# Differential attention in a four-layer trunk: value evacuation in pairs, a second room for the cast of queries and keys, rotation from the scaled copy, exponentials tied behind aT

## The chip, the cores and the metric

One Trainium2 chip (trn2), one of its cores. The metric is the device time of one execution in microseconds (us); smaller is better. All inputs and outputs are fp32. Matrix products are formed in three passes: each factor is split into a high part (type fp32r) and the low rest, and high x high, high x low and low x high are added up in PSUM.

## What is computed

The program is a trunk of four layers over a sequence of 512 tokens and 1024 channels; each has a mixer and a gated feed-forward part. The mixers are S5, gated linear attention, differential attention, S5. The change touches the third only, whose reference is, cut to its core:

```python
def diff_attn_mixer(h, positions, w_qkv, lam_q1, lam_k1, lam_q2, lam_k2, subln_g, w_o, lambda_init):
    q, k, v = jnp.split(h @ w_qkv, 3, axis=-1)
    q = partial_rope(q.reshape(bsz, seq, 16, 64), positions) * 64 ** -0.5
    k = partial_rope(k.reshape(bsz, seq, 16, 64), positions)
    v = v.reshape(bsz, seq, 8, 128)
...
        s = jnp.einsum('bqhd,bkhd->bhqk', qb, k)
        p = jax.nn.softmax(jnp.where(mask, s, NEG_INF), axis=-1)
        p = p.reshape(bsz, 8, 2, 128, seq)
        a = p[:, :, 0] - lam * p[:, :, 1]
        return jnp.einsum('bhqk,bkhd->bqhd', a, v)
...
    o = o * lax.rsqrt(jnp.mean(o * o, axis=-1, keepdims=True) + 1e-5) * subln_g * (1.0 - lambda_init)
    return o.reshape(bsz, seq, 1024) @ w_o
```

There are 8 heads of two softmaxes each. partial_rope rotates the first 16 of every 64 channels by tables of cosines and sines of the position.

## The kernel before

Everything below lies in the method diff (L2171 to L2500) and the few helpers that it calls. The layer input hT stands transposed in SBUF as a high and a low half; r is the row factor of the norm that precedes the layer. A "unit" is three matmuls (high x high, high x low, low x high) into one PSUM bank.

**Projections.** project(hf, z) computes 512 columns of queries (z = 0) or keys (z = 1) for half hf of the heads, in four banks of 128 tokens each (acc, four banks in all). When a bank is complete, evac empties it twice: ACT writes the copy scaled by r (qtm, L2237), and DVE reads the bank again for the rotation (ro, L2242 with cosines, L2245 twice with sines, from tables cos2r and sin2r that carry r already, made at L2205), and puts the rotated 16 columns into qtm (L2248). Six units later TensorE transposes qtm (L2253), and ACT copies the result to qk (L2254). Values for the first four heads come from project(0, 2); those for the others from values_of (L2386), which puts two blocks of 128 tokens into one bank, 256 columns each, and has ACT empty each half as soon as it is complete (vall, L2391). At the last k the matmuls of the second half of the bank follow on those of the first.

**Preparing a head.** prepare(j) has ACT write the high half of queries and keys (hl, L2273, 128x1024), DVE the low half (L2274), and then POOL issue eight DMAs (qs, L2281, four of 128 KB; ks, L2282, four of 256 KB) that lay the two softmaxes' rows out for the score matmuls. hl has one room, but for head 1, which takes one from the pool of weight halves (whl, five rooms, which holds ks as well). The cast of the next head writes that room, so it waits for the eight DMAs that read it. Head 4 and those after it use the second half of the projections, which are made beside steps 0 to 9.

**The 32 steps.** Step i stands for head j = i // 4 and query block t = i % 4. In a step TensorE's order is: turned(i), four transposes of the probabilities a (aTp, L2321), copied by ACT (aT, L2323); values(i - 1), the product with the values (op, L2331), copied by ACT (o_s, L2334) and squared for the norm (junk, L2336); at t = 2, prepare(j + 2); then scores(i + 2), four matmuls (L2299), for each softmax a DVE pass that adds the mask and takes the minimum (L2303, with nm) and an exponential on ACT (pr, L2307), then DVE's small steps (L2309, L2310) and the combination of the two softmaxes (pr, L2314); last, beside[i] units of other products (projections, then values, then the output product wo, whose first columns are ready from the first heads on). When a head is complete, normalised(j) forms its norm on DVE (L2343, L2344), a power on POOL (L524), and scales o_s on DVE (L2347); two steps later done transposes it (oTp, L2354), which ACT and DVE split into oT (L529, L530). done stands in the middle of the units of its step; in step 30 it stands right behind the scores, ahead of the first pair of units for the output.

In PSUM, the banks are acc (four), s (two) and two slots for everything that is transposed, which aTp, op, oTp and qTp share.

**What sets the order.** TensorE runs this layer in the order written in the code (self.hand). ACT, DVE, POOL and SP run in an order that a scheduler sets at build time from its own costs, with due times for what has to go first; issue_after(x) tells it that an instruction stands behind x on its engine. The weight halves of the products (whl) are made by ACT (L405) and DVE (L413) out of the staged weights (wst).

**Behind the steps.** values(31), the norm of head 7, the pairs of output units for two token blocks, the last oT, the other two blocks, and then the feed-forward part of the layer.

Of the kernel before, what the change touches and what calls it, by code (L numbers as in the profile page):

```python
# [22 lines left out]
P = 128  # L23
# [302 lines left out]
class Trunk:  # L326
# [1844 lines left out]
    def diff(self, l, left, after):  # L2171
# [4 lines left out]
        with self.tc.tile_pool(name="diff", bufs=1) as p:  # L2176
# [18 lines left out]
                nc.sync.dma_start(sg[:], i["diff_subln"][0].partition_broadcast(P))  # L2195
                v.tensor_scalar_mul(sg[:], sg[:], 1.0 - LAMBDA_INIT)

            cos2 = p.tile([P, NT, 16], F32, name="cos2r")
            sin2 = p.tile([P, NT, 16], F32, name="sin2r")

            def factors():

                left.finish()
                for o, y in ((cos2, self.cos2), (sin2, self.sin2)):
                    v.tensor_tensor(o[:], y[:], r[:].unsqueeze(2).broadcast_to([P, NT, 16]), op=ALU.mult)  # L2205

            self.pend.append(factors)

            stat = lambda k, part, t: hT[part][:, k, t * P : (t + 1) * P]

# [21 lines left out]
            def project(hf, z):  # L2232
                qk = qks[hf]

                def evac(t, ps):
                    q = self.np_.tile([P, 512], F32, tag=("h", "hh")[t % 2], name="qtm", bufs=2)
                    nc.scalar.mul(q[:], ps[:], r[:, t : t + 1])  # L2237
                    s3 = ps[:].rearrange("p (h d) -> p h d", d=64)
                    q3 = q[:].rearrange("p (h d) -> p h d", d=64)
                    ro = p.tile([P, 2, 8, 16], F32, tag="ro", name="ro", bufs=2)  # L2240
                    c2 = cos2[:, t].unsqueeze(1).broadcast_to([P, 8, 16])
                    v.tensor_tensor(ro[:, 0], s3[:, :, 0:16], c2, op=ALU.mult)  # L2242
                    for y in range(2):
                        s1 = sin2[:, t, y * 8 : y * 8 + 8].unsqueeze(1).broadcast_to([P, 8, 8])
                        v.tensor_tensor(  # L2245
                            ro[:, 1, :, y * 8 : y * 8 + 8], s3[:, :, 8 - 8 * y : 16 - 8 * y], s1, op=ALU.mult
                        )
                    v.tensor_tensor(q3[:, :, 0:16], ro[:, 0], ro[:, 1], op=ALU.add)  # L2248

                    def turn():  # L2250
                        tp = self.tp("qTp")
                        for j in range(4):
                            nc.tensor.transpose(tp[:, j], q[:, j * P : (j + 1) * P], self.ident[:])  # L2253
                        nc.scalar.copy(qk[:, z, :, t * P : (t + 1) * P], tp[:])  # L2254

                    queue.append((clock[0] + 6, turn))

                def evac_v(t, ps):
                    nc.scalar.mul(vall[0][:, t, hf * 512 : (hf + 1) * 512], ps[:], r[:, t : t + 1])

                if z == 2 and not vall:
                    vall.append(self.xp.tile([P, NT, D], F32, tag="x", name="vall"))
                yield from self.gemm_units(stat, w, KT, z * D + hf * 512, evac_v if z == 2 else evac)
# [3 lines left out]
            def prepare(j):  # L2267


                room, bufs, tag = (self.wp, 5, "whl") if j == 1 else (p, 1, "hl")  # L2270
                hl = room.tile([P, 2, 2, SEQ], F32R, tag=tag, name="hl", bufs=bufs)
                src = qks[j // 4][:, :, j % 4]
                nc.scalar.copy(hl[:, 0], src)  # L2273
                v.tensor_tensor(hl[:, 1], src, hl[:, 0].bitcast(F32), op=ALU.subtract)  # L2274
# [15 lines left out]
            def scores(i):  # L2290
                j, t = divmod(i, NT)
                ts = slice(t * P, (t + 1) * P)
                qs, ks = ready[j]
                st = kept[j][0]
                pr, sums = [], self.sp.tile([P, 4], F32, tag="sums", name="sums", bufs=4)
                ss = [self.sbank("s"), self.sbank("s")]
                for m in range(2):
                    for z in range(2):
                        nc.tensor.matmul(ss[m][:], qs[:, m, ts], ks[:, m, z], start=z == 0, stop=z == 1)  # L2299
                for m in range(2):  # L2300
                    e = T("pr", 4)
                    nm = self.sp.tile([P, 1], F32, tag="nm", name="nm", bufs=4)
                    v.tensor_tensor_reduce(  # L2303
                        e[:], ss[m][:], mask[:, t], -0.125, 3e38, op0=ALU.add, op1=ALU.min, accum_out=nm[:]
                    )
                    sum_ = st[:, 0, t : t + 1] if m == 0 else sums[:, 1:2]
                    nc.scalar.activation(e[:], e[:], AF.Exp, scale=-1.0, bias=nm[:], accum_out=sum_)  # L2307
                    pr.append(e)
                v.reciprocal(sums[:, 2:3], sums[:, 1:2])  # L2309
                v.tensor_scalar(  # L2310
                    sums[:, 3:4], st[:, 0, t : t + 1], sums[:, 2:3], self.neglam[:], op0=ALU.mult, op1=ALU.mult
                )
                a = pr[0]
                v.scalar_tensor_tensor(a[:], pr[1][:], sums[:, 3:4], pr[0][:], op0=ALU.mult, op1=ALU.add)  # L2314
                soft[i] = a

            def turned(i):
                a = soft.pop(i)
                tp = self.tp("aTp")
                for kt in range(4):  # L2320
                    nc.tensor.transpose(tp[:, kt], a[:, kt * P : (kt + 1) * P], self.ident[:])  # L2321
                aT = p.tile([P, 4, P], F32, tag="aT", name="aT", bufs=2)
                nc.scalar.copy(aT[:], tp[:])  # L2323
                return aT

            def values(i, aT):
# [48 lines left out]
            def values_of(c0):  # L2375

                banks = [self.acc(), self.acc()]
                for kb in range(0, KT, 4):
                    src = w[kb * P : (kb + 4) * P, 2 * D + c0 : 2 * D + c0 + 256]
                    hl = self.weights(src.rearrange("(a p) n -> p a n", p=P), 4, 256)  # L2380
                    for a in range(4):
                        k = kb + a
                        for t in range(NT):
                            o = banks[t // 2][:, (t % 2) * 256 : (t % 2 + 1) * 256]
                            for n, (x, y) in enumerate(((0, 0), (0, 1), (1, 0))):
                                nc.tensor.matmul(  # L2386
                                    o, stat(k, x, t), hl[:, y, a], start=not (k or t % 2 or n),
                                    stop=k == KT - 1 and n == 2, skip_group_check=True,
                                )
                            if k == KT - 1:  # L2390
                                nc.scalar.mul(vall[0][:, t, c0 : c0 + 256], o, r[:, t : t + 1])  # L2391
                            if t % 2:
                                yield

# [30 lines left out]
            def pair(k):  # L2425
                for t in range(2):
                    unit(t, k)
# [3 lines left out]
            for i in range(32):  # L2431
# [12 lines left out]
                if i < 30:  # L2444
                    scores(i + 2)
                if i == 30:
                    done.pop(i)()
                    banks = [self.sbank("acc1"), self.sbank("acc1")]
                    pair(0)
                run(units, beside[i] // 2)  # L2450
                if i in done:
                    done.pop(i)()
                run(units, beside[i] - beside[i] // 2)
                if i == 16:
                    back(0)
                if i == 20:
# [4 lines left out]
            values(31, aT)  # L2461
            last_head = normalised(7)
            back(1)
            for k in range(1, KT - 1):
                if k == KT - 2:
                    last_head()
                pair(k)
# [78 lines left out]
```

## Time and profile before

| | |
|---|---|
| three runs | 2276.57 us median (2271.59 to 2281.54) |
| profiled execution | 2276.01 us, of which the span is 2274.2 us |
| mean granted TensorE clock | 0.995 |
| attention layer | about 1150 to 1427 us of the span |

Busy time by engine in stretches of the layer, us (the granted clock and the DMA share stand at the end of a row):

| stretch | PE | DVE | ACT | POOL | PE clock | DMA |
|---|---|---|---|---|---|---|
| 1150 to 1240 (90 us) | 90.00 | 39.34 | 40.29 | 13.45 | 1.00 | 0.59 |
| 1240 to 1275 (35) | 33.44 | 22.02 | 21.62 | 5.50 | 1.00 | 0.42 |
| 1275 to 1300 (25) | 24.12 | 15.59 | 18.29 | 5.54 | 1.00 | 0.30 |
| 1300 to 1325 (25) | 19.23 | 16.68 | 17.04 | 5.58 | 0.93 | 0.67 |
| 1325 to 1350 (25) | 22.03 | 18.37 | 18.14 | 9.70 | 1.00 | 0.78 |
| 1350 to 1375 (25) | 24.32 | 19.39 | 18.43 | 3.10 | 1.00 | 0.37 |
| 1375 to 1395 (20) | 16.95 | 14.66 | 13.59 | 1.00 | 1.00 | 0.26 |
| 1395 to 1430 (35) | 35.00 | 18.81 | 18.15 | 7.05 | 1.00 | 0.70 |

How to read the profile: times are us from the start of the span. PE is TensorE's matmuls, PEld its weight loads, DVE VectorE, ACT ScalarE, POOL GpSimd, SP SyncE. L2307 is line 2307 of the kernel. A row of groups has the line, engine, operation, what it writes and from what, the shape, how often, the busy time, the mean duration in ns, and the idle time just ahead of it with what ended it. A row of waits has who waited, for whom, us in total, how often, and the longest.

### The profile page before, as it was taken

The page shows a single profiled execution, that of the slowest core. Times are in us where ns is not written, and L with a number is a line of the kernel's source. Part 1 is how long each engine was busy: PE and PEld are TensorE (multiplying, and loading weights), DVE is VectorE, ACT ScalarE, POOL GpSimd, SP SyncE. Part 2 cuts the span into 40 slices and gives each one's busy share as a digit, 9 for nine tenths or more (in the row PEclk, how much of TensorE's full clock was granted, in tenths as well). Part 3 has the DMA queues.
Part 4 walks back from the last instruction along what each step waited for, and adds up shares of the span by engine and source line. Part 5 has one row for each costly group of instructions (what it writes and reads, how often), then busy time and mean ns, then how long its engine had stood idle before and what let it go on. Part 6 is the DMA issues. An engine that isn't in the chain of part 4 may idle for free. (4 is left out here: it accounts for less than half of the span.)

```text
span 2274.2 us, 37366 instructions
## 1 busy us (share of the span) xinstructions
PE 2193.2 (96%) x14967; PEld 1964.7 (86%) x14967; DVE 1580.3 (69%) x2413; ACT 1112.7 (49%) x1773; POOL 319.0 (14%) x432
## 2 busy tenths in 40 slices
PE   6999999999999999999999989999999899999998
PEld 5888889989777799999988877989999788989997
DVE  9955878777435488776745576976766965957675
ACT  8534535445433365564435675644534224635343
POOL 5301141430000010100002121110000000101000
PEclk9999999999999999999999999999999999999999
DMA  4356657763322567765337365886642555866632
GB/s 90 63 169 167 179 150 181 180 169 90 104 84 65 148 158 190 183 169 139 102 126 167 75 149 139 231 206 147 166 103 56 139 154 146 202 166 158 167 75 75
DMA packets 295527, 319.92 MB, mean 141 GB/s; under 512 B 70141, under 2 KB 235289, under 8 KB 295226
## 3 DMA queue, kind: packets, MB, share of 16 engines
q1 hardware_dynamic: 232730, 235.79, 34.5%
q0 software_dynamic: 62624, 81.75, 19.3%
q8 instruction: 118, 1.93, 0.4%
q14 instruction: 55, 0.45, 0.1%
HBM read 285.62 MB, written 16.65 MB: 133 GB/s over the span
## 5 line engine op out<-in xcount | busy, mean ns | idle before, releaser
L413 DVE TENSOR_TENSOR whl<-wst,whl 128x1024 fp32r<-128x1024 f32 x272 | 331.6, 1223 | 278.7 <-ACT whl L405 276.2
L405 ACT CAST whl<-wst 128x1024 fp32r<-128x1024 f32 x272 | 284.4, 1050 | 343.0 <-PE acc L435 246.5
L576 PE MATMUL a<-side,whl 128*128 128x256 f32 x3168 | 383.5, 277 | 7.5 <-DVE whl L413 6.0
L576 PEld LDWEIGHTS a<-side,whl 128*128 128x128 f32 x3168 | 370.6, 188 | 10.0 <-DVE whl L413 6.7
L433 PE MATMUL acc<-whl,act 128*128 128x512 f32 x704 | 275.9, 392 | 1.5 <-DVE g L621 1.2
L435 PE MATMUL acc<-whl,act 128*128 128x512 f32 x704 | 274.5, 390 | 0.0
L434 PE MATMUL acc<-whl,act 128*128 128x512 f32 x704 | 274.5, 390 | 0.0
L576 PE MATMUL c<-side,whl 128*128 128x256 f32 x2112 | 255.0, 277 | 3.3 <-DVE whl L413 3.3
L576 PEld LDWEIGHTS c<-side,whl 128*128 128x128 f32 x2112 | 246.9, 188 | 4.2 <-DVE whl L413 4.1
L413 DVE TENSOR_TENSOR whl<-slot,whl 128x1024 fp32r<-128x1024 f32 x105 | 127.7, 1221 | 66.5 <-ACT whl L405 66.5
L433 PEld LDWEIGHTS acc<-whl,act 128*128 128x128 f32 x704 | 132.1, 188 | 30.7 <-DVE g L621 1.6
L435 PEld LDWEIGHTS acc<-whl,act 128*128 128x128 f32 x704 | 132.2, 188 | 27.7
L405 ACT CAST whl<-slot 128x1024 fp32r<-128x1024 f32 x105 | 110.0, 1052 | 92.2 <-PE acc L435 46.3
L434 PEld LDWEIGHTS acc<-whl,act 128*128 128x128 f32 x704 | 132.2, 188 | 26.0
L576 PE MATMUL d<-sides,whl 128*128 128x256 f32 x1056 | 133.6, 283 | 2.6 <-ACT whl L405 2.6
L576 PEld LDWEIGHTS d<-sides,whl 128*128 128x128 f32 x1056 | 128.9, 191 | 3.4 <-ACT whl L405 3.4
L576 PE MATMUL a<-sides,whl 128*128 128x256 f32 x1056 | 129.1, 278 | 2.0 <-DVE whl L413 1.2
L433 PE MATMUL acc<-whl,hT 128*128 128x512 f32 x320 | 128.9, 403 | 1.3 <-DVE ro L2245 1.3
L576 PEld LDWEIGHTS a<-sides,whl 128*128 128x128 f32 x1056 | 124.9, 188 | 3.3 <-DVE whl L413 1.4
L435 PE MATMUL acc<-whl,hT 128*128 128x512 f32 x320 | 125.6, 393 | 0.0
L434 PE MATMUL acc<-whl,hT 128*128 128x512 f32 x320 | 125.5, 392 | 0.0
L612 POOL DMA_DIRECT2D wst<-in_ffn_w_gate_up_dram x44 | 57.0, 1295 | 442.4 <-DMA wst<-in_ffn_w_gate_up_dram 149.9
(458 smaller groups left out, 3942.8 us busy)
## 6 DMA issues: line engine op xcount, KB each, us to landing
wst<-in_ffn_w_gate_up_dram SPq DMA_DIRECT2D x88, 512.0 KB, 4.6
wst<-in_ffn_w_down_dram SPq DMA_DIRECT2D x88, 512.0 KB, 4.8
slot<-in_ffn_w_gate_up_dram SPq DMA_DIRECT2D x69, 512.0 KB, 5.7
wst<-in_ffn_w_gate_up_dram POOLq DMA_DIRECT2D x44, 512.0 KB, 6.0
halves<-in_ffn_w_gate_up_dram SPq DMA_DIRECT2D x42, 512.0 KB, 5.5
wst<-in_s_w_glu_dram SPq DMA_DIRECT2D x32, 512.0 KB, 5.3
wst<-in_gla_w_in_dram SPq DMA_DIRECT2D x24, 512.0 KB, 3.7
wst<-in_diff_w_qkv_dram SPq DMA_DIRECT2D x24, 512.0 KB, 4.9
```

The source lines that it names most:

```text
L405: self.last["high"] = self.nc.scalar.copy(hl[:, 0], w[:])
L413: self.last["low"] = self.nc.vector.tensor_tensor(hl[:, 1], w[:], hl[:, 0].bitcast(F32), op=ALU.subtract)
L433: mm(out, lh, rh, start=first, stop=False)
L434: mm(out, lh, rl, start=False, stop=False)
L435: self.last["mm"] = mm(out, ll, rh, start=False, stop=last)
L576: mm(o, hl[:, x, k, c], side[:, y, k], start=first and not (j or k or n), stop=k == 3 and n == 2, skip_group_check=True,)
L612: nc.gpsimd.dma_start(w[:], left.quarter(*plus, b), accum_op=ALU.add)
```

## The change

It has five parts, all in diff.

- *Rotation from the scaled copy.* DVE's rotation reads qtm, which ACT has scaled by r, and no longer the PSUM bank; the tables are then the plain ones, and cos2r and sin2r go (two DVE instructions). The two halves of ro lie in one tile kept for the whole layer.
- *Two rooms for the cast.* hl has two rooms of its own for all heads; head 1 no longer takes one of whl's.
- *Exponentials behind aT.* From the second step on, the exponentials of scores(i + 2) may not be put ahead of aT(i) on ACT.
- *Values in pairs.* ACT empties both halves of a bank when the second is complete.
- *The place of done.* It stands directly behind the scores of its step, with all units behind it; in step 30 one pair of output units stands ahead of it and a second one behind it, so that the pairs after the steps begin at 2 and not at 1.

```diff
-            cos2 = p.tile([P, NT, 16], F32, name="cos2r")
-            sin2 = p.tile([P, NT, 16], F32, name="sin2r")
-
-            def factors():
-
-                left.finish()
-                for o, y in ((cos2, self.cos2), (sin2, self.sin2)):
-                    v.tensor_tensor(o[:], y[:], r[:].unsqueeze(2).broadcast_to([P, NT, 16]), op=ALU.mult)
-
-            self.pend.append(factors)
+            self.pend.append(left.finish)
+            turns = self.np_.tile([P, 512], F32, tag="R", name="ro", bufs=1)
+            ros = [turns[:, 256 * n : 256 * n + 256].rearrange("p (z h d) -> p z h d", z=2, h=8) for n in range(2)]
...
-                    s3 = ps[:].rearrange("p (h d) -> p h d", d=64)
                     q3 = q[:].rearrange("p (h d) -> p h d", d=64)
-                    ro = p.tile([P, 2, 8, 16], F32, tag="ro", name="ro", bufs=2)
-                    c2 = cos2[:, t].unsqueeze(1).broadcast_to([P, 8, 16])
-                    v.tensor_tensor(ro[:, 0], s3[:, :, 0:16], c2, op=ALU.mult)
+                    ro = ros[t % 2]
+                    c2 = self.cos2[:, t].unsqueeze(1).broadcast_to([P, 8, 16])
+                    v.tensor_tensor(ro[:, 0], q3[:, :, 0:16], c2, op=ALU.mult)
...
-                room, bufs, tag = (self.wp, 5, "whl") if j == 1 else (p, 1, "hl")
-                hl = room.tile([P, 2, 2, SEQ], F32R, tag=tag, name="hl", bufs=bufs)
+                hl = p.tile([P, 2, 2, SEQ], F32R, tag="hl", name="hl", bufs=2)
...
-                    nc.scalar.activation(e[:], e[:], AF.Exp, scale=-1.0, bias=nm[:], accum_out=sum_)
+                    with self.tc.issue_after(self.last_aT.ins) if i > 1 else nullcontext():
+                        nc.scalar.activation(e[:], e[:], AF.Exp, scale=-1.0, bias=nm[:], accum_out=sum_)
...
-                nc.scalar.copy(aT[:], tp[:])
+                self.last_aT = nc.scalar.copy(aT[:], tp[:])
...
-                            if k == KT - 1:
-                                nc.scalar.mul(vall[0][:, t, c0 : c0 + 256], o, r[:, t : t + 1])
+                            if t % 2 and k == KT - 1:
+                                for y in (t - 1, t):
+                                    o = banks[t // 2][:, (y % 2) * 256 : (y % 2 + 1) * 256]
+                                    nc.scalar.mul(vall[0][:, y, c0 : c0 + 256], o, r[:, y : y + 1])
...
                 if i == 30:
-                    done.pop(i)()
                     banks = [self.sbank("acc1"), self.sbank("acc1")]
                     pair(0)
-                run(units, beside[i] // 2)
                 if i in done:
                     done.pop(i)()
-                run(units, beside[i] - beside[i] // 2)
+                if i == 30:
+                    pair(1)
+                run(units, beside[i])
...
-            for k in range(1, KT - 1):
+            for k in range(2, KT - 1):
```

In the changed kernel the lines from L2205 on stand seven to nine lower in number: the cast is L2264, its low half L2265, the scores L2290, the mask L2294, the exponential L2299, pr L2306, aTp L2313, aT L2315, op L2323, oTp L2346, the value products L2378 and their copies L2385.

More of the change, by code (lines that the diff above doesn't have):

```diff
@@ L2237, in evac @@
                     nc.scalar.mul(q[:], ps[:], r[:, t : t + 1])
-                    s3 = ps[:].rearrange("p (h d) -> p h d", d=64)
                     q3 = q[:].rearrange("p (h d) -> p h d", d=64)
-                    ro = p.tile([P, 2, 8, 16], F32, tag="ro", name="ro", bufs=2)
-                    c2 = cos2[:, t].unsqueeze(1).broadcast_to([P, 8, 16])
-                    v.tensor_tensor(ro[:, 0], s3[:, :, 0:16], c2, op=ALU.mult)
+                    ro = ros[t % 2]
+                    c2 = self.cos2[:, t].unsqueeze(1).broadcast_to([P, 8, 16])
+                    v.tensor_tensor(ro[:, 0], q3[:, :, 0:16], c2, op=ALU.mult)
                     for y in range(2):
-                        s1 = sin2[:, t, y * 8 : y * 8 + 8].unsqueeze(1).broadcast_to([P, 8, 8])
+                        s1 = self.sin2[:, t, y * 8 : y * 8 + 8].unsqueeze(1).broadcast_to([P, 8, 8])
                         v.tensor_tensor(
-                            ro[:, 1, :, y * 8 : y * 8 + 8], s3[:, :, 8 - 8 * y : 16 - 8 * y], s1, op=ALU.mult
+                            ro[:, 1, :, y * 8 : y * 8 + 8], q3[:, :, 8 - 8 * y : 16 - 8 * y], s1, op=ALU.mult
                         )
```

## The prediction

> **What bounds the kernel now.** I read the page first, then the view of who waited for whom on PE, cut to 1140–1425 us, where the attention layer lies. From the page:
>
> ```profile
> span 2274.2 us, 37366 instructions
> ...
> PE 2193.2 (96%) x14967; PEld 1964.7 (86%) x14967; DVE 1580.3 (69%) x2413; ACT 1112.7 (49%) x1773; POOL 319.0 (14%) x432
> ...
> PE 38%; DVE 3%; ACT 2%; DMA 1%; issue 1%; POOL 0%; DVEq 0%; POOLq 0%; ACTq 0%
> ```
>
> PE is busy 96% of the span, and matmuls lead the chain that ended last. PE's instructions are as many after the change as before, so what the change can win is idle time of PE inside this layer, and what it can lose is new idle time there. The waits of PE in the layer:
>
> ```profile
> PE acc L2386 <- ACT vall L2391: 4.1, 4, 1.7
> PE aTp L2321 <- DVE pr L2314: 4.0, 1, 4.0
> PE op L2331 <- ACT aT L2323: 2.9, 4, 0.9
> PE op L2331 <- DVE oT L530: 1.4, 1, 1.4
> PE acc L433 <- DVE ro L2245: 1.3, 1, 1.3
> PE oTp L2354 <- ACT aT L2323: 1.0, 1, 1.0
> PE op L2331 <- ACT qk L2254: 0.2, 1, 0.2
> ```
>
> They sum to 14.9 us: the stock from which every gain must come. One thing is to be added. After the longest wait the matmuls themselves are slow; from the PE rows in order of time, and the 5 us window at that place (its last figures are granted clock, DMA share, GB/s):
>
> ```profile
> 1295.85 1.16 PE L2331 MATMUL op<-vall,aT 128*128 128x128 f32 x8 [0.88 <-ACT aT L2323]
> 1296.77 1.18 PE L2299 MATMUL s<-ks,qs 128*128 128x512 f32 x4
> ...
> 1310.73 0.63 PE L2321 MATMUL aTp<-ident,pr 128*128 128x128 f32 x4 [4.00 <-DVE pr L2314]
> 1311.19 1.79 PE L2331 MATMUL op<-vall,aT 128*128 128x128 f32 x8
> 1312.63 2.05 PE L2299 MATMUL s<-ks,qs 128*128 128x512 f32 x4
> ```
>
> ```profile
> 1310.00:1315.00 5.00, 4.27 (x19) 3.83 (x19) 3.83 (x9) 3.29 (x9) 3.26 (x6) 0.66 0.96 182
> ```
>
> A row has start, duration, and in brackets the idle time ahead of it with what ended it. The eight op matmuls begin 1.44 us before the scores (1311.19 to 1312.63) where 0.92 is usual (1295.85 to 1296.77), and four score matmuls take 2.05 instead of 1.18: together 1.4 too long. The granted clock is 0.66 over the window, (1 - 0.66) x 5 = 1.7 if all of it counts. I take 1.7, since the matmuls behind the scores are in the window too. The stock is 14.9 + 1.7 = 16.6 us, 0.73% of the time.
>
> **Part by part**, in order of time. The orders named are those in which the changed program issues on each engine.
>
> *Rotation from the scaled copy, and the third cast.* The next projection's first matmul needs a PSUM bank that the rotation on DVE still reads:
>
> ```profile
> 1242.21 0.39 PE L433 MATMUL acc<-whl,hT 128*128 128x512 f32 x1
> ...
> 1244.03 0.39 PE L435 MATMUL acc<-whl,hT 128*128 128x512 f32 x1
> 1245.74 0.47 PE L433 MATMUL acc<-whl,hT 128*128 128x512 f32 x1 [1.33 <-DVE ro L2245]
> ```
>
> ```profile
> 1236.18 1.05 ACT L2273 CAST hl<-qk 128x1024 fp32r<-128x1024 f32 x1 [2.07 <-DMA qs<-hl]
> ...
> 1295.22 0.58 ACT L2323 COPY aT<-aTp 128x512 f32<-128x512 f32 x1
> ...
> 1306.15 1.05 ACT L2273 CAST hl<-qk 128x1024 fp32r<-128x1024 f32 x1 [3.41 <-DMA ks<-hl]
> ```
>
> DVE was late because ACT had stood 2.07 us in front of a cast whose only room was still being copied out. With two rooms that cast stands earlier, and the bank is free once ACT has scaled it, whatever DVE does. Nearly all of the 1.33 goes: **gain 1.3** (ends 0 and 1.5, with the 0.2 behind it). Next is the transpose of the rotated tile, two units later. A unit is three matmuls; the eight starts from 1242.21 to 1244.03 give 0.2275 each, so a unit is 0.68 and the cover 1.37 us. The two table products that go lie beside PE and are costed at nothing.
>
> *The cast for head 5.* With a second room it no longer waits, and the order puts it straight behind the cast for head 4, ahead of an aT copy (the one at 1295.22) on an ACT that is then without a gap. That copy frees the PSUM slot for the op at 1295.85, which waited 0.88 for it; now it waits about 0.88 + 0.95 (a cast of 1.05, less 0.1 of overlap with its neighbour) = 1.83: **loss 0.95** (ends 0, and 2.2 where the low half on DVE, 1.22 in the rows below, holds up the exponentials ahead of that copy as well). With the cast go its low half and the eight DMAs of head 5 on POOL's queue; the first two of them come ahead of the power of head 2's norm:
>
> ```profile
> 1302.12 1.03 POOL L524 TENSOR_TENSOR rs<-q,mhalf 128x4 f32<-128x4 f32 x1 [5.74 <-DVE q L2344]
> ```
>
> POOL stood idle 5.74 us ahead of it, so two issues there cost nothing; if that cover went, the norm of head 2 would be late by an issue or two, and its transposes have a whole step to spare.
>
> *The cast for head 6, at the longest wait.* These are the groups by line, and the view of tile ks over 1275–1312:
>
> ```profile
> L2307 ACT ACTIVATE pr<-pr,nm 128x512 f32<-128x512 f32 x64 | 45.8, 716 | 14.6 <-DVE nm L2303 14.5
> ...
> L2273 ACT CAST hl<-qk 128x1024 fp32r<-128x1024 f32 x8 | 8.4, 1048 | 12.1 <-DMA ks<-hl 5.6 <-PE acc L435 4.4 <-DMA qs<-hl 2.1
> ...
> L2391 ACT ACTIVATE vall<-acc,rcol 128x256 f32<-128x256 f32 x8 | 3.7, 470 | 2.9 <-PE acc L2386 2.9
> ```
>
> ```profile
> L2303 DVE CUSTOM_DVE_ANT_0 pr<-s,mask 128x512 f32<-128x512 f32 x64 | 42.3, 686 | 22.4 <-PE s L2299 22.3
> ...
> L2314 DVE SCALAR_TENSOR_TENSOR pr<-pr,sums 128x512 f32<-128x512 f32 x32 | 24.0, 751 | 1.0
> L2274 DVE TENSOR_TENSOR hl<-qk,hl 128x1024 fp32r<-128x1024 f32 x8 | 9.8, 1224 | 18.4 <-ACT hl L2273 16.8 <-DMA qs<-hl 1.6
> ...
> L2310 DVE TENSOR_SCALAR sums<-st,sums,neglam 128x1 f32<-128x1 f32 x32 | 8.7, 273 | 1.1
> ...
> L530 DVE TENSOR_TENSOR oT<-oTp,oT 128x512 fp32r<-128x512 f32 x8 | 5.5, 684 | 3.6 <-ACT oT L529 3.6
> ```
>
> ```profile
> DMA to landing us min/median/max: 3.1/4.6/10.1
> ```
>
> In the kernel before, the cast for head 5 waits until 1306.15 for the copies of head 4 out of the single room, between the two exponentials of step 14; all behind it on ACT (exponentials, aT) and DVE stands. The change doesn't remove this wait: now the cast for *head 6* needs the room of head 4, and waits for the same copies. But it stands behind both exponentials of step 14. From the landing: cast 1.05, low half 1.22, the factor 0.27, one mask 0.69, pr 0.75, less some 0.1 of overlap, ends near 1310.05 instead of 1310.73. PE would be there at 1310.73 - 4.00 = 1306.73, and comes 0.95 later for the loss above, at 1307.7. The wait is about 2.35 instead of 4.0: **gain 1.65**. Its ends are a copy that lands early (nothing left, gain 4.0) and one that lands later (rival 2).
>
> *The clock behind it.* A wait of 4.00 dropped the clock; none of the others, up to 1.72, did. At 2.35 I take it to stay: **gain 1.7** (ends 0 and 1.7), on the side of the nearer row, 1.72. [...]
>
> *Values in pairs.* Here the second half of a bank waits for ACT to empty the first half:
>
> ```profile
> 1318.31 0.63 PE L2386 MATMUL acc<-whl,hT 128*128 128x256 f32 x3 [1.20 <-ACT vall L2391]
> ...
> 1345.92 0.98 PE L2386 MATMUL acc<-whl,hT 128*128 128x256 f32 x6 [1.72 <-ACT vall L2391]
> ```
>
> In pairs, nothing writes a bank while it is read: all 4.1 go. In place of them four copies (4 x 0.47 = 1.88) stand together on ACT ahead of an aT, and the second exponential of step 15 stands behind it; from these durations I expect 0.6 at aTp(15) and 0.2 at the next op: **gain 3.3** (ends 2 and 4.1).
>
> *Step 26 and the end.* oTp goes directly behind the scores, and in step 30 behind one pair:
>
> ```profile
> 1376.99 1.16 PE L2331 MATMUL op<-vall,aT 128*128 128x128 f32 x8 [1.37 <-DVE oT L530]
> ...
> 1390.73 0.66 PE L2354 MATMUL oTp<-ident,o_s 128*128 128x128 f32 x4 [1.01 <-ACT aT L2323]
> ...
> 1393.89 1.16 PE L2331 MATMUL op<-vall,aT 128*128 128x128 f32 x8 [0.67 <-ACT aT L2323]
> ```
>
> In step 26 oTp comes a unit (0.68) earlier, but ACT's copy of it still stands behind two exponentials: **gain 0.5** (ends 0 and 1.37). In step 30 the pair (six matmuls, 1.37) covers the 1.01, and pair 1 covers most of the next wait, of which some 0.5 is left on L530: **gain 1.2** (ends 0 and 1.7). For the last head only pairs 2 to 5 remain ahead, four of 1.37 = 5.5 us, to hide the norm and scaling of its o_s. I take that as enough; the other end is 1.37 lost, if the pair that moved ahead was all needed. The remaining op waits (0.68 each at two places) keep their order: nothing.
>
> Sum: 1.3 - 0.95 + 1.65 + 1.7 + 3.3 + 0.5 + 1.2 = 8.7 us. The profiled execution took 2276.0 (span 2274.2 and 1.8 around it), 0.6 below the median of the three runs, 2276.57. **Forecast 2276.0 - 8.7 = 2267.3**, 0.38% less. With the worse end of the two most doubtful terms (1.25 more lost at the cast of head 5, 1.3 less from the values) and half of the last two (0.85) it is 2270.7; with nothing lost at that cast (0.95), all of the values (0.8), of step 26 (0.87) and of step 30 (0.5) and the first ones (0.2) it is 2264.0.
>
> **Rivals.**
> 1. *Every wait goes.* The early casts find slack and the copies land early. For it: the median landing is 4.6 us, not 10.1. Against it: two 0.68 waits have the same order. Between 14 and 16.6 us go, from 2262 to 2259.4: about 2260.5.
> 2. *The copies land later.* The copies for head 5 now follow on POOL's queue while those for head 4 run; two of them, 0.5 MB, at the 182 GB/s of the window above are 2.8 us if they share. Then the wait is 2.35 + 2.8 = 5.1, and the clock falls again: 2267.3 + 2.8 + 1.7 = 2271.8. Against it: one queue, head 4 first.
> 3. *Given back behind the layer.* After it, DVE bounds:
>
> ```profile
> 1470.00:1480.00 10.00, 7.56 (x61) 6.97 (x60) 9.88 (x13) 6.27 (x9) 2.55 (x2) 1.00 1.13 294
> ```
>
> PE idles 2.4 us there with DVE at 9.88 of 10. If PE arrives earlier than weights and DVE, about half of the gain is lost: 2272.
> 4. *Slower: the tie.* Exponentials of step i+2 may no longer pass aT(i). pr is ready ahead of PE now (DVE, then PE, in order of time):
>
> ```profile
> 1300.32 0.75 DVE L2314 SCALAR_TENSOR_TENSOR pr<-pr,sums 128x512 f32<-128x512 f32 x1
> ```
>
> ```profile
> 1302.88 0.60 PE L2321 MATMUL aTp<-ident,pr 128*128 128x128 f32 x4
> ```
>
> pr of step 13 ends at 1301.07 on DVE, and PE's aTp takes it at 1302.88: 1.8 us of slack, in a stretch without stalls. If aT comes so late that the tie uses up more than that, each step waits for it; one exponential, 0.72, in each of the steps 14 to 25 is 8.6 us, and the 5.0 us of the last three terms are lost in the same place: 2267.3 + 8.6 + 5.0 = 2280.9. For it: aT lies between exponentials in a crowded ACT. Against it: an exponential behind aT needs only 0.7 of the 1.8.
>
> **How the numbers follow.** Forecast 0.55, rival 1 0.17, rival 2 0.12, rival 3 0.06, rival 4 0.10. The forecast's own range is 2264 to 2271. The range is 2259 to 2278: rival 1 in full, rivals 2 and 3, and the start of rival 4. A difference of 0.5% (11.4 us) is about what a measurement of this kernel can tell from no change. Faster by more than that (under 2264.6): rival 1 and a sixth of the forecast (its lower edge, 2264, lies there), 0.26. Slower by more than that: the upper part of rival 4, 0.08. The same: 0.66.
>
> **What would show it.** In the profile after: no wait of acc on vall and none on ro; the wait of op in step 11 grown to about 1.8; aTp(14) waiting some 2.4 us on pr, the head 6 cast before it waiting for ks, and granted clock 1.00 in the 5 us behind. A wait there of over 3 with a low clock is rival 2. Waits of aTp on pr in several steps between 1315 and 1375 are rival 4. The PE idle of the layer falling as said while 1430–1500 idles longer is rival 3. I am wrong in the sum if a wait appears that none of these names, such as scores waiting for ks.

## The result and the profile after

The changed kernel takes 2267.49 us (median of 7 runs, 2264.01 to 2269.6) against 2274.75 (7 runs, 2268.84 to 2281.54): the ratio on record is 0.9964, with a 95% interval of 0.9952 to 0.9977. That is 8.2 us (5.2 to 10.9); the two medians by themselves lie 7.3 us apart. 8.7 was forecast. The profiled execution took 2264.01. Its page begins:

```profile
span 2262.1 us, 37360 instructions
...
PE 2191.7 (97%) x14967; PEld 1963.9 (87%) x14967; DVE 1580.2 (70%) x2411; ACT 1111.5 (49%) x1773; POOL 317.9 (14%) x432
...
PE 48%; DVE 3%; ACT 2%; issue 1%; DMA 1%; POOL 0%; DVEq 0%; POOLq 0%; ACTq 0%; SPq 0%
```

The waits of PE in the layer (1130 to 1425 us), to be laid beside the seven rows of before:

```profile
PE op L2323 <- ACT aT L2315: 3.0, 3, 1.7
PE aTp L2313 <- DVE pr L2306: 1.9, 1, 1.9
PE op L2323 <- DVE oT L530: 1.7, 2, 1.4
PE op L2323 <- ACT qk L2246: 0.2, 1, 0.2
```

14.9 us have become 6.8. The waits on vall and on ro are gone. To measure the layer by itself I take its stretch from the first score matmul to the first matmul of the feed-forward part. From the view of the scores' line (first and last start are its fourth column) and PE's rows in order of time, before and then after:

```profile
L2299 PE MATMUL s<-ks,qs x128: 387/397/774, 1213.8 to 1387.3; 128*128 128x512 f32 x128
```

```profile
1425.46 2.91 PE L576 MATMUL a<-sides,whl 128*128 128x256 f32 x24
```

```profile
L2290 PE MATMUL s<-ks,qs x128: 387/397/481, 1212.7 to 1377.2; 128*128 128x512 f32 x128
```

```profile
1413.73 2.91 PE L576 MATMUL a<-sides,whl 128*128 128x256 f32 x24
```

The stretch fell from 211.7 to 201.0, by 10.6: 8.1 of waits and 2.5 beside them. The low clock of before makes up at most 1.7 of the 2.5 (0.66 over 5 us); where the other 0.8 lies isn't shown. The longest single score matmul shows the low clock too, 774 ns before and 481 after. The other 1.4 us between the two profiled executions (12.0 in all) lie outside: 1.1 ahead of the stretch, whose start varies from 1211.1 to 1215.6 over all the profiles below, and 0.3 behind it, where nothing was changed. What is left of the waits, in order of time:

```profile
1294.04 1.16 PE L2323 MATMUL op<-vall,aT 128*128 128x128 f32 x8 [1.69 <-ACT aT L2315]
...
1306.78 0.63 PE L2313 MATMUL aTp<-ident,pr 128*128 128x128 f32 x4 [1.85 <-DVE pr L2306]
...
1366.82 1.16 PE L2323 MATMUL op<-vall,aT 128*128 128x128 f32 x8 [1.41 <-DVE oT L530]
...
1383.55 1.16 PE L2323 MATMUL op<-vall,aT 128*128 128x128 f32 x8 [0.32 <-DVE oT L530]
```

Each is at a place that the prediction named. The wait of aTp(14), 1.85, has another cause than it gave. On ACT, on DVE and on POOL (the cast of head 6, what stands ahead of pr(14), and the power that DVE waits for):

```profile
1301.55 1.03 ACT L2264 CAST hl<-qk 128x1024 fp32r<-128x1024 f32 x1
...
1306.00 0.72 ACT L2299 ACTIVATE pr<-pr,nm 128x512 f32<-128x512 f32 x1 [1.41 <-DVE nm L2294]
```

```profile
1302.83 1.14 DVE L2339 SCALAR_TENSOR_TENSOR o_s<-o_s,rs,sg 128x128 f32<-128x128 f32 x4 [0.93 <-POOL rs L524]
1303.89 0.17 DVE L2301 RECIPROCAL sums<-sums 128x1 f32<-128x1 f32 x1
1303.96 1.22 DVE L2265 TENSOR_TENSOR hl<-qk,hl 128x1024 fp32r<-128x1024 f32 x1
...
1305.27 0.69 DVE L2294 CUSTOM_DVE_ANT_0 pr<-s,mask 128x512 f32<-128x512 f32 x1
...
1305.88 0.76 DVE L2306 SCALAR_TENSOR_TENSOR pr<-pr,sums 128x512 f32<-128x512 f32 x1
```

```profile
1300.92 1.88 POOL L524 TENSOR_TENSOR rs<-q,mhalf 128x4 f32<-128x4 f32 x1 [5.98 <-DVE q L2336]
```

The cast has no bracket: ACT did not wait for the copies of head 4 at all. DVE is late by its own queue: a wait of 0.93 for POOL's power, then the scaling of head 2 (1.14), the low half of head 6 (1.22) and a mask (0.69), all ahead of pr(14), though its exponentials were through at 1301.6. Only the mask and the low half had been counted. The power took 1.88 us here and 1.03 in the kernel before (at 1302.12); no run tests why.

### The profile page after: what moved, and what is told of

Same layout as the page of the kernel before. It is cut to its first block, busy times and chain, and to the rows that moved or that the text cites. A ratio compares the mean times of both kernels' runs of the same rounds, so it can differ in the third digit from the quotient of the medians.

```text
span 2262.1 us, 37360 instructions
## 1 busy us (share of the span) xinstructions
PE 2191.7 (97%) x14967; PEld 1963.9 (87%) x14967; DVE 1580.2 (70%) x2411; ACT 1111.5 (49%) x1773; POOL 317.9 (14%) x432
## 4 chain that ended last, share of the span: by engine, by line
PE 48%; DVE 3%; ACT 2%; issue 1%; DMA 1%; POOL 0%; DVEq 0%; POOLq 0%; ACTq 0%; SPq 0%
PE a L576 10%; PE acc L433 8%; PE acc L435 8%; PE acc L434 8%; PE c L576 5%; PE d L576 3%; PE y L1481 1%; PE op L2323 1%; PE s L2290 1%; DVE whl L413 1%; PE acc L2378 1%; ACT whl L405 1%; PE V L1445 1%; PE tp L116 0%; DMA wst<-in_ffn_w_gate_up_dram 0%
```

## The experiments

The theory behind them: each part earns back the wait that it removes, and the second room does so at aTp(14). The rivals: the second room does nearly all, or the long wait of before was chance. In the table, "stretch" is as above, "waits" the sum of PE's waits in the layer, "rest" the stretch less these waits, "clock" the granted clock in 10 us windows from 1300 to 1380 where it was not 1.00, and the ratio is to the kernel before.

| kernel | stretch | waits | rest | clock | ratio (95%) |
|---|---|---|---|---|---|
| before | 211.7 | 14.9 | 196.8 | 0.83 | 1 |
| before, second profile | 211.2 | 12.7 | 198.5 | 0.83, 0.83 | - |
| changed | 201.0 | 6.8 | 194.2 | | 0.9964 (0.9952 to 0.9977) |
| changed, without the tie | 202.3 | 6.7 | 195.6 | 0.88, 0.95 | 0.9968 (0.9957 to 0.9980) |
| single room | 203.1 | 8.3 | 194.8 | | 0.9964 (0.9952 to 0.9977) |
| rotation from PSUM | 201.9 | 7.7 | 194.2 | | 0.9969 (0.9958 to 0.9981) |
| values one by one | 206.7 | 10.6 | 196.1 | 0.87, 0.96 | 0.9987 (0.9976 to 0.9999) |
| done in the middle | 204.5 | 9.7 | 194.8 | | 0.9985 (0.9975 to 0.9994) |
| before + second room | 208.1 | 12.9 | 195.2 | | 0.9995 (0.9984 to 1.0005) |
| later casts | 201.2 | 5.4 | 195.8 | 0.83 | 0.9955 (0.9938 to 0.9973) |
| copy ahead of exponentials | 195.6 | 2.4 | 193.2 | | 0.9940 (0.9919 to 0.9961) |
| both | 200.6 | 4.9 | 195.7 | 0.83 | 0.9957 (0.9943 to 0.9972) |
| copy ahead, single room | 197.4 | 3.0 | 194.4 | | 0.9948 (0.9932 to 0.9963) |
| copy ahead, without its tie | 195.9 | 2.4 | 193.5 | | 0.9941 (0.9922 to 0.9960) |

**Single room put back.**

```diff
-                hl = p.tile([P, 2, 2, SEQ], F32R, tag="hl", name="hl", bufs=2)
+                room, bufs, tag = (self.wp, 5, "whl") if j == 1 else (p, 1, "hl")
+                hl = room.tile([P, 2, 2, SEQ], F32R, tag=tag, name="hl", bufs=bufs)
```

> The changed kernel with the single room for the cast put back (head 1 again in a room of the weight halves); all other parts stay. Theory: the second room removes the long wait of aTp(14) and the low clock behind it, and costs 0.8 at the op of step 11; the wait on the rotation is removed by the rotation alone. Then aTp(14) waits about 4.0 again (1.85 in the changed kernel), the clock falls (1.7), the op of step 11 waits 0.88 and not 1.69, and no wait of acc on ro is seen: 4.0 - 1.85 + 1.7 - 0.8 = 3.0 us slower than the changed kernel, about 2270.5. Rival: it was the early cast of head 3, and so the room, that removed the wait on the rotation: then about 1.3 more stands at the projection's first matmul, on ACT's copy of the bank, 2271.8. Rival two: the copies of head 4 land early in this run, and the wait is 2 us or less with full clock: about 2267.

Measured: 0.9964, the same ratio as with two rooms; the stretch is 2.1 longer. The second rival holds at the long wait: the cast waits for the copies again, but PE then waits 2.06 and the clock stays at 1.00. ACT's row, then PE's rows:

```profile
1302.94 1.05 ACT L2265 CAST hl<-qk 128x1024 fp32r<-128x1024 f32 x1 [1.47 <-DMA ks<-hl]
```

```profile
1244.40 0.50 PE L433 MATMUL acc<-whl,hT 128*128 128x512 f32 x1 [0.27 <-ACT qtm L2230]
...
1307.52 0.63 PE L2314 MATMUL aTp<-ident,pr 128*128 128x128 f32 x4 [2.06 <-DVE pr L2307]
```

So the second room takes 0.2 from the long wait. The place of the rotation keeps its gain without the room (0.27 left). The stretch is longer by new waits for aT, 1.1 and 0.6 at two later places, and these the time doesn't show.

**Rotation from PSUM.** In evac, the rotation reads ps with cos2r and sin2r again; the tile ros stays.

```diff
-                    c2 = self.cos2[:, t].unsqueeze(1).broadcast_to([P, 8, 16])
-                    v.tensor_tensor(ro[:, 0], q3[:, :, 0:16], c2, op=ALU.mult)
+                    c2 = cos2[:, t].unsqueeze(1).broadcast_to([P, 8, 16])
+                    v.tensor_tensor(ro[:, 0], s3[:, :, 0:16], c2, op=ALU.mult)
```

> The changed kernel with the rotation reading the PSUM bank again, with the scaled tables; the tile for the two halves stays where the change put it, and the second room stays. Theory: ACT no longer stands 2.07 us in front of the cast of head 3, so DVE is on time and the wait of acc on ro is under 0.4: no measurable difference, +0.2, about 2267.7. Rival: the bank is free only when DVE has read it twice, and DVE has its pr in front of that; the wait is 1.0 to 1.3 as before: about 2268.7, seen as a wait of acc on ro in the trace.

Measured: the rival. With the cast of head 3 early, PE still waits 0.98 for DVE to read the bank:

```profile
1244.63 0.47 PE L433 MATMUL acc<-whl,hT 128*128 128x512 f32 x1 [0.98 <-DVE ro L2247]
```

Of the 1.33, 1.0 is the rotation's. The rest may be the cast's, but it isn't shown: the second profile of the kernel before, below, has 1.1 at this place with nothing changed. In time, 1 us can't be told (0.9969 against 0.9964).

**Values one by one.**

```diff
-                            if t % 2 and k == KT - 1:
-                                for y in (t - 1, t):
-                                    o = banks[t // 2][:, (y % 2) * 256 : (y % 2 + 1) * 256]
-                                    nc.scalar.mul(vall[0][:, y, c0 : c0 + 256], o, r[:, y : y + 1])
+                            if k == KT - 1:
+                                nc.scalar.mul(vall[0][:, t, c0 : c0 + 256], o, r[:, t : t + 1])
```

> The changed kernel with each half bank of values emptied as soon as it is complete. Theory: the four waits of acc on vall come back whole, 4.1 us, for nothing stood in their place in the changed kernel: about 2271.6. Rival: ACT comes earlier to them without the casts that stood in front, and they are half as long, 2 us: about 2269.5.

Measured: 0.9987, stretch 5.7 longer. The theory, and more: 4.5 us of waits where the value products stand, and a drop of the clock (0.87 and 0.96 over 10 us each, 1.7 us) where two of them lie close together (2.03 and 0.70).

```profile
PE acc L2378 <- ACT vall L2383: 3.9, 3, 2.0
PE op L2323 <- ACT aT L2315: 2.4, 2, 1.7
PE aTp L2313 <- DVE pr L2306: 1.8, 1, 1.8
PE op L2323 <- DVE oT L530: 1.7, 2, 1.4
PE acc L2378 <- DVE sums L2302: 0.6, 1, 0.6
```

**done in the middle.**

```diff
                 if i == 30:
+                    done.pop(i)()
                     banks = [self.sbank("acc1"), self.sbank("acc1")]
                     pair(0)
+                run(units, beside[i] // 2)
                 if i in done:
                     done.pop(i)()
-                if i == 30:
-                    pair(1)
-                run(units, beside[i])
+                run(units, beside[i] - beside[i] // 2)
...
-            for k in range(2, KT - 1):
+            for k in range(1, KT - 1):
```

> The changed kernel with the transposes of a finished head in the middle of the units again, and in step 30 right behind the scores. Theory: step 26 waits 1.4 with either place (1.37 before, 1.41 in the changed kernel), since ACT's copy stands behind both exponentials anyway; step 30 waits 1.0 + 0.7 instead of 0.3: 1.4 us slower, about 2268.9. Rival: in step 26 the later place adds its unit of 0.68: 2.0 us slower, 2269.5.

Measured: 0.9985, stretch 3.4 longer, more than either said. Steps 26 and 30 are as the theory has them, but behind the transposes of step 14, a place that nobody had named, the op waits for L530:

```profile
1314.87 1.16 PE L2323 MATMUL op<-vall,aT 128*128 128x128 f32 x8 [1.63 <-DVE oT L530]
```

**The kernel before, a second profile.**

> The kernel before, unchanged, once more. With the single room put back in the changed kernel, the cast of head 5 stood in the same place of ACT's order, but the copies of head 4 were there 12.5 us after their first issue, not 14.4, aTp(14) waited 2.06 and not 4.00, and the clock stayed full. Theory: the landing varies from run to run, and 4.00 with a low clock was one long run: this look shows a wait of 2 to 3 and granted clock 1.00 behind it, and a time of 2271 to 2274. Rival: the wait belongs to the kernel before, because head 1's room among the weight halves or the order of the copies holds them up there: 4.0 again with a clock of 0.66 and 2275 to 2277.

Measured: 2275.89 us, the time of the first profile, by another way. The wait of aTp(14) is 2.2, with a clock of 1.00 right behind it, as the theory says. The time isn't, for the clock fell twice, both times behind two waits for vall: 0.56 and 1.19, and 1.53 and 0.57. Below are PE's waits, PE's rows at these places, the first issue of the copies of head 4 with the cast that waits for them (in the first profile 1291.70 and 1306.15), and two 5 us windows:

```profile
PE acc L2386 <- ACT vall L2391: 3.9, 4, 1.5
...
PE aTp L2321 <- DVE pr L2314: 2.2, 1, 2.2
```

```profile
1314.24 0.80 PE L2386 MATMUL acc<-whl,hT 128*128 128x256 f32 x3 [1.19 <-ACT vall L2391]
...
1343.30 0.98 PE L2386 MATMUL acc<-whl,hT 128*128 128x256 f32 x6 [1.53 <-ACT vall L2391]
1344.85 0.70 PE L2386 MATMUL acc<-whl,hT 128*128 128x256 f32 x3 [0.57 <-ACT vall L2391]
```

```profile
1291.03 1.09 POOL L2281 DMA_DIRECT2D qs<-hl  x2 [12.16 <-ACT hl L2273]
```

```profile
1303.69 1.05 ACT L2273 CAST hl<-qk 128x1024 fp32r<-128x1024 f32 x1 [1.62 <-DMA ks<-hl]
```

```profile
1345.00:1350.00 5.00, 5.00 (x23) 4.64 (x24) 2.95 (x5) 3.18 (x7) 0.36 (x1) 0.66 0.53 97
1340.00:1345.00 5.00, 2.89 (x19) 2.31 (x18) 4.08 (x15) 3.91 (x13) 3.41 (x5) 1.00 0.65 129
```

**Later casts.**

```diff
-                nc.scalar.copy(hl[:, 0], src)
+                with self.tc.issue_after(self.last_aT.ins) if j > 4 else nullcontext():
+                    nc.scalar.copy(hl[:, 0], src)
```

> The changed kernel with the casts of heads 5, 6 and 7 held behind aT of steps 14, 18 and 22. Theory: what is left at steps 11 and 14 is the price of casts pulled too far ahead, on ACT in step 11 (1.69 against 0.88) and on DVE in step 14 (the low half of head 6 ahead of pr(14), 1.85): both shrink, 0.8 + 1.85 = 2.6 us faster than the changed kernel, about 2264.9. Rival: the casts only move to a place as crowded; the values' copies stand next to the cast of head 5, and weight halves come later, so 1 to 3 us of new waits appear between steps 15 and 24: 2266 to 2268.

Measured: 0.9955, stretch 201.2, no better than the changed kernel. Both waits shrink as the theory says (0.88 at step 11, none at aTp(14)), and the rival's new ones come: 0.64 and 1.04 for weight halves, 0.68 for oT, within 5 us, and the clock falls behind them:

```profile
1311.26 1.16 PE L2324 MATMUL op<-vall,aT 128*128 128x128 f32 x8 [0.68 <-DVE oT L530]
...
1313.98 0.39 PE L2379 MATMUL acc<-whl,hT 128*128 128x256 f32 x1 [0.64 <-ACT whl L405]
1315.41 2.96 PE L2379 MATMUL acc<-whl,hT 128*128 128x256 f32 x16 [1.04 <-DVE whl L413]
```

```profile
1315.00:1320.00 5.00, 4.59 (x26) 4.59 (x27) 2.69 (x5) 2.09 (x4) 0.00 (x0) 0.66 0.93 235
```

**Copy ahead of the exponentials.** split_t keeps its copy as last_split.

```diff
-            def scores(i):
+            def scores(i, mid=None):
...
+                tie = self.last_aT.ins if i > 1 else None
+                if mid:
+                    mid()
+                    tie = self.last_split.ins
...
-                    with self.tc.issue_after(self.last_aT.ins) if i > 1 else nullcontext():
+                    with self.tc.issue_after(tie) if tie else nullcontext():
...
-                    scores(i + 2)
+                    scores(i + 2, done.pop(i, None))
```

> The changed kernel with the transposes of a finished head issued between the score matmuls and the softmax, and the exponentials of that step held behind ACT's copy of them. Theory: the op of step 26 waits 1.41 because the copy (ACT) stands behind two exponentials and its low half (DVE) behind pr: with the copy ahead it waits under 0.3, 1.1 to 1.4 us faster than the changed kernel, about 2266.2. Rival: the exponentials are late by the copy (0.57) in eight steps, and a wait of aTp on pr in step 14 or 15 grows by as much: no gain, 2267.5.

Measured: 0.9940, 2261.93 us; the stretch is 5.4 shorter than in the changed kernel, four times what the theory had. With its twin below it has the lowest ratio of all versions tried. It is clearly faster than the kernel before; its interval (0.9919 to 0.9961) still touches that of the changed kernel. Its waits of PE, and the op of step 11:

```profile
PE op L2327 <- DVE oT L530: 1.5, 3, 0.7
PE aTp L2317 <- DVE pr L2310: 0.7, 1, 0.7
...
PE op L2327 <- ACT qk L2246: 0.2, 1, 0.2
```

```profile
1295.09 1.16 PE L2327 MATMUL op<-vall,aT 128*128 128x128 f32 x8 [0.69 <-DVE oT L530]
```

The wait behind the transposes of step 26 is gone, and so are the 3.0 us for aT in steps 11, 19 and 23. What ends the waits tells the slots: in the changed program op takes there the PSUM slot of the aTp just issued, and waits for its copy (1.69 for aT in step 11); in this one it takes the slot of oTp, and waits 0.69 or less for L530. The low half of head 6 is issued behind pr(14), and aTp(14) waits 0.66. The rival's later exponentials show nowhere.

**Both.**

> Both of the last two edits together. Theory: their gains add up, 2.6 + 1.2 = 3.8 us faster than the changed kernel, about 2263.7. Rival: the waits of steps 14 and 15 are the same exponentials seen twice, and the gain is that of the larger one alone, 2264.9 or more.

Measured: 0.9957, 2266.73 us, stretch 200.6. The gains don't add up; the time is the rival's (2264.9 or more), but not for its reason. The waits for weight halves grow to 1.22 and 1.50 and the clock falls (0.83 from 1310 to 1320): the later casts cost what the copy gains.

**Without the tie to aT.**

```diff
-                    with self.tc.issue_after(self.last_aT.ins) if i > 1 else nullcontext():
-                        nc.scalar.activation(e[:], e[:], AF.Exp, scale=-1.0, bias=nm[:], accum_out=sum_)
+                    nc.scalar.activation(e[:], e[:], AF.Exp, scale=-1.0, bias=nm[:], accum_out=sum_)
```

> The changed kernel without the tie of the exponentials to aT. Every engine is given the same instructions in the same order as in the changed kernel, so the tie does nothing, and this is a second look at the changed kernel. Theory: from the first score matmul to the first matmul of the feed-forward part 201 us (201.0 in the changed kernel, 211.7 and 211.2 in the two looks at the kernel before), the same waits to 0.1, and a ratio of 0.996 to the kernel before. Rival: the waits vary with the landing of copies from run to run, and the stretch differs by over 1 us.

Measured: 0.9968, the same waits to 0.1; the stretch 1.3 longer, past the 1 us of the rival, but not by waits. The 1.85 of aTp(14) dropped the clock this time. PE's rows and the window:

```profile
1307.28 0.89 PE L2312 MATMUL aTp<-ident,pr 128*128 128x128 f32 x4 [1.85 <-DVE pr L2305]
1307.97 1.91 PE L2322 MATMUL op<-vall,aT 128*128 128x128 f32 x8
1309.53 1.81 PE L2290 MATMUL s<-ks,qs 128*128 128x512 f32 x4
```

```profile
1305.00:1310.00 5.00, 3.15 (x17) 2.98 (x16) 4.12 (x10) 2.30 (x7) 1.55 (x4) 0.75 1.16 244
```

**The second room alone**, in the kernel before:

```diff
-                room, bufs, tag = (self.wp, 5, "whl") if j == 1 else (p, 1, "hl")
-                hl = room.tile([P, 2, 2, SEQ], F32R, tag=tag, name="hl", bufs=bufs)
+                hl = p.tile([P, 2, 2, SEQ], F32R, tag="hl", name="hl", bufs=2)
```

(The tile ro lies where the change puts it, which frees the space for the room.)

> The kernel before with the second room for the cast alone (the two halves of the rotation's tile moved to the place that the change gives them, to make room). Theory: the room by itself is worth little: the wait on ro is 1.0 (1.3 before), the op of step 11 waits 1.7 (0.9), aTp(14) 1.85 (2.2 to 4.0), the four waits on vall stand, and a wait on L530 of 1.6 comes in step 14: the stretch from the first score matmul to the feed-forward part is 208 to 211 (211.2 and 211.7 before), 0 to 3 us faster. Rival: the room is what the change lives on, and the stretch falls by 4 us or more, to under 207.5.

Measured: 0.9995, no difference. The stretch of 208.1 is the lower end of the theory; its profiled execution had the clock at 1.00 from 1300 to 1380. The wait behind the transposes of step 14 did not come.

**Copy ahead, with the single room.** The first edit above, in that kernel.

> The kernel with the copy ahead of the exponentials (stretch 195.6) with the single room put back. Theory: the room is still worth some 2 us in the stretch, as it was in the changed kernel (203.1 against 201.0), since the cast of head 5 again waits for the copies of head 4 ahead of aT: aTp(14) or an op behind it waits 1 to 2.5, stretch 197 to 198.5. Rival: with the exponentials of step 14 ahead of the cast nothing waits on it, and the stretch is 195.6 or less, for the early casts have gone.

Measured: stretch 197.4, inside the theory (197 to 198.5), but the waits (1.01 for oT behind step 14, 0.33 for aT, and 0.7, 0.5 and 0.3 at the three old places) make only 0.6 of its 1.8; aTp(14) doesn't wait. In time, 0.9948 against 0.9940, the intervals overlap: what the room is worth in this kernel stays open.

**Copy ahead, without its tie.** The line tie = self.last_split.ins is left out.

> The kernel with the transposes between scores and softmax, without the tie of the exponentials to ACT's copy: in heads 2, 5 and 7 the copy now stands between the two exponentials. Theory: the gain came from where DVE's low half stands, and half an exponential is enough to bring a wait back: 0.3 to 0.9 in step 26, stretch 196 to 196.5. Rival: the position of the transposes on TensorE made the gain by itself, and the stretch is 195.6 to 0.2.

Measured: the rival, though the stretch of 195.9 is 0.1 past what it allowed; no wait in step 26. The place of the transposes on TensorE makes the gain, not the tie.

## Why the prediction was right, and where it wasn't

The time (2267.3 forecast, 2267.49 measured) and the main mechanism were right: waits of PE in one layer, taken away or moved. That the two times agree to 0.2 us is luck: the forecast starts from the profiled 2276.0, 1.3 above the later median of 2274.75, and its terms miss in both directions. Step by step, the gain forecast and that of the two profiles:

| step | forecast | measured | |
|---|---|---|---|
| rotation and third cast | 1.3 | 1.3 | the rotation's own is 1.0, shown by undoing it |
| cast for head 5 | -0.95 | -0.8 | 1.69 for 0.88, at the place named |
| cast for head 6, the long wait | 1.65 | 2.15 | by another cause |
| clock behind it | 1.7 | 2.5 | all that isn't waits; the clock is at most 1.7 of it |
| values in pairs | 3.3 | 4.1 | the 0.8 at aTp(15) and op(14) did not come |
| step 26 | 0.5 | 0.0 | failed |
| step 30 | 1.2 | 1.4 | |
| sum | 8.7 | 10.6 | 8.2 by the ratio, 7.3 between the medians |

**"DVE was late because ACT had stood 2.07 us in front of a cast"** was at most a small part of the reason: with that cast early, PE still waited 0.98 for DVE. The gain holds because the bank no longer waits for DVE at all.

**"The cast for head 6, at the longest wait" failed in its working.** I took the landing at 1306.15 for a fixed thing of the kernel. In the first profile the cast began 14.4 us after the first issue of the copies (1291.70); it began 12.7 after it in the second profile (1291.03 to 1303.69) and 12.5 with the single room, and PE waited 2.2 and 2.1. So some 1.8 of the 4.00, and a drop of the clock at this place, were that run's, not the kernel's (the second profile lost as much at other places); the change takes 0.2 to 0.4 from the wait in the other two. What it leaves is DVE's queue, of which I had counted two of four pieces.

**"At 2.35 I take it to stay" failed as a rule.** A wait of 1.85 dropped the clock without the tie (0.75 from 1305 to 1310) and not in the changed kernel, whose engines have the same order (1.00 there); 1.53 and 0.57 dropped it in the second profile of the kernel before (0.66 from 1345 to 1350), 1.72 and 0.57 at the same place in the first did not (1.00). The size of a wait alone doesn't tell whether the 1.7 is lost. The timed runs hardly show it: the mean granted clock of a run is 0.9953 on average over 49 runs of the kernel before and 0.9955 over 14 of the changed program, with and without the tie. That is about 0.4 us, where one drop of 1.7 us is 0.0007.

**Step 26** went as its own sentence says: the copy stands behind two exponentials. I still gave it 0.5; it was 0. What the new place of done earned lies behind step 14, where the middle place costs 1.6 in the changed kernel. In the kernel before, the op at that place, by the same order of slots, follows the same L530, but comes behind PE's waits for vall (1.20 just ahead) and doesn't wait; no row showed the price, and I had none for it.

**The tie** could not be a rival: the instructions of every engine stand in the same order without it.

That the sum came out is in part luck: the profile of before had a long landing in it, which I counted as a gain, while other terms gave more than I had said. In time, undoing one part at a time, the values cost 5.2 us (0.9987 against 0.9964) and the place of done 4.8 (0.9985), where the sum had 3.3 and 1.7. The second room had 2.4 in the sum with its clock term (1.65 + 1.7 - 0.95), and the time shows nothing of it (0.9964 without it). In the same set of runs the medians are 2270.98 and 2269.84 against 2264.36 with the single room, so the order is clear; the sizes are rough, for each ratio is uncertain by some 2.7 us. Rivals 1, 2 and 3 did not come (6.8 us of waits are left; the cast of head 6 waited for no copy; the feed-forward part took the time it took: 848.7 us from its first matmul to the end before, 848.4 after). How long the landing is in the timed runs of either kernel stays open, since only the profiled executions have rows.

## What to carry to other kernels

Take two profiles of the kernel before, ahead of pricing a wait that a DMA ends: the same copies were there 14.4 us after their first issue in one and 12.7 in the other. When a part of a change moves casts earlier, add up everything that the consumer's queue then holds ahead of the late instruction, scaling and powers included, and not only what was moved. Removing several short waits that lie close together can be worth more than their sum (undoing the pairs of values brought back 3.8 us of waits and 5.7 us of stretch), and a version with fewer waits (the later casts, 5.4 us for 6.8) can be no faster where the ones left lie in a row (0.9955 for 0.9964).

## What the runs showed of the hardware

The granted clock fell behind one long wait (4.00 in the kernel before, 0.66 in the 5 us from 1310) and behind groups of short ones (0.68, 0.64 and 1.04 within 5 us with the later casts, 0.66 in the 5 us from 1315). Seven drops lie inside the layer in the fourteen profiles, and the windows lose 1.7 us to each (0.17 of 10 us). The one in the kernel before begins at 1311.33 and lasts 3.41 us at a clock of 0.50, so it costs at most 1.7 us (0.34 of a 5 us window). Over the whole of a trace the drops begin 175, 196, 137 and 144 times 3.413 us apart in the kernel before, and 72, 103, 329 and 144 times in the changed one.

With the layer divided into stretches of that length, counted from the drops, PE was idle for 2.81 us in the stretch ahead of the drop of the kernel before (busy 0.60 of 3.41, from 1307.92 to 1311.33). The most in any other stretch from 1130 to 1430 was 1.62 there (from 1314.74) and 1.54 in the changed kernel (from 1303.06), and no drop came behind either. The 1.85 of aTp(14) lay across an edge in the changed kernel, 1.54 in one stretch and 0.31 in the next. Without the tie, it ended at 1307.28. There the clock was 0.75 from 1305 to 1310 and 0.91 in the next 5 us, which at half the clock is 3.4 us from about 1307.5, so the whole wait lay in the 3.41 us ahead of the drop. That it matters where a wait falls is my estimate from the profiles with and without the tie; no run moves a wait to test it.

With the clock at 1.00 from 1300 to 1380 the stretch from the scores to the feed-forward part, less its waits, was 193.2 to 195.2 in eight kernels; with drops it was 195.6 to 198.5 in the other six profiles.
